# Attention of a hybrid trunk: value products of a unit in one block, probabilities divided by their sums on GpSimd

## The chip, the core and the metric

The kernel runs on one NeuronCore of a Trainium2 chip. The core has a matrix engine (TensorE, PE in the profile), VectorE (DVE), ScalarE (ACT), GpSimd (POOL) and a queue engine that issues most loads (SyncE, SP). Each engine takes its instructions strictly in the order in which they were put into its queue, and waits at semaphores for the others. Matrix products and transposes are written into PSUM (eight banks of 128 x 512 floats); GpSimd is given no PSUM operand anywhere in this kernel. The metric is the device time of one execution in microseconds (us).

## The reference, cut to what matters

Two trunk layers with three parallel mixers (pooling, gated linear attention, softmax attention), an output projection and an MLP, on 512 latent and 256 context tokens of width 1024. The change touches the softmax attention alone: 8 query heads of 64, which share 2 key/value heads.

```python
def gqa_attend(qb, k, v):
    s = jnp.einsum('bqhgd,bkhd->bhgqk', qb, k, preferred_element_type=jnp.float32) * HEAD_DIM ** -0.5
    p = jax.nn.softmax(s, axis=-1)
    return jnp.einsum('bhgqk,bkhd->bqhgd', p.astype(v.dtype), v)
...
    mix = jnp.concatenate([pool_mixer(p, w_pool, s_pool),
                           gla_output(o_gl, gg, g_gla, x.dtype),
                           latent_attention(ql, k_all, v_all)], axis=-1) @ w_out
```

Latent queries see all 768 keys (latent and context); context queries, which only the first layer has, see the 256 context keys.

## The kernel before

**Units.** The attention of a layer is cut into units: one pair of heads (`hp`, 0 to 3) times 256 queries. A latent unit (`q0` 0 or 2) has four tiles of 128 queries x 768 keys (two heads, two query blocks). A context unit (`q0` 4, first layer only) has four tiles of 128 x 256. The first layer has 8 latent and 4 context units, the second has 8 latent ones.

**Softmax part (L1009).** For each tile of a latent unit TensorE writes the scores into a PSUM buffer of two banks (`sc`, L1033 and L1034; the queries are held as high and low parts one above the other, so that the products with the high and the low part of the keys make up the whole). VectorE takes the row maximum (`nmx`, L1036), ScalarE the exponential, whose row sums come out beside it (`p` and `sm`, L1037). There are two such PSUM buffers (`psA`), so the scores of the tile after next wait for the exponential of this one. After the four tiles VectorE takes the reciprocal of the four sums (L1039). A context unit does the same with one PSUM tile for all four (L1019 to L1025).

**Value part (L1043).** The probabilities must lie with the keys on the partitions. For each block of 128 keys TensorE transposes the four tiles into one bank (`pT`, L1054), and ScalarE (even blocks, L1064) or VectorE (odd blocks, L1066) copies it to SBUF (`pe`). The blocks go in pairs: two blocks are transposed and copied, and then multiplied with the values of their keys into one accumulator (`av`, L1071; two products for each block, one for each head, into the upper and the lower 64 partitions). After the last pair four small matmuls spread the reciprocal sums over the partitions (`rb`, L1078), ScalarE copies the result (L1082), VectorE multiplies (`f`, L1084), ScalarE makes the high part of the mix (L1086) and GpSimd the low part (L1087). Each float32 matmul of `av` and `rb` appears as two instructions in the profile.

**Interleaving.** `att_thread` steps the softmax part of unit n and, after each step, one step of the value part of unit n-1: transposes and products of one pair beside each score tile, the end with `rb` beside the reciprocal. Before the first unit of a pair of heads, `q_stack` (L1093) transposes and splits the queries. In the early part of the attention the steps of gated linear attention run between (an order string, `STEPS`, says how); the pooling runs between the units. The framework puts the instructions into the queues by priority in the order of the program, with a timing estimate of its own, and sets all waits; the order within a queue is fixed before the run.

**Buffers.** The probability tiles take four of five buffers of the weight tags `hi` and `lo`, by turns. The copies `pe` of a pair share one tile of the tag `raw`, of which there are three, and which the weight loads use too (`wload`, L152). The copies of the last unit of a layer lie in other slots, so that the three `raw` buffers come free for the loads of the output projection's weights (`w_out`), which follow the attention. `psB` (one bank each: `pT`, `rb`, `qT`, `op`) has three buffers, the accumulator `av` has one. `sub_lo` (L78) is VectorE's subtraction that makes the low part of a split value.

Of the kernel before, what the change touches and what calls it, by code (L numbers as in the profile page):

```python
# [10 lines left out]
F32 = mybir.dt.float32  # L11
F32R = mybir.dt.float32r
I32 = mybir.dt.int32
AF = mybir.ActivationFunctionType
ALU = mybir.AluOpType
# [19 lines left out]
def hybrid_kernel(ctx, tc, x, c, cx, c_ctx, w_mod, b_mod, g_mix, w_in, w_pool, s_pool, w_gate, b_gate,  # L35
                  g_gla, g_q, g_k, w_out, g_mlp, w_up, w_down, g_final, k_mask, k_rope, k_edge, k_invw, out):
    nc = tc.nc
    V, A, G, T = nc.vector, nc.scalar, nc.gpsimd, nc.tensor
# [13 lines left out]
    def nm(s):  # L52
        uid[0] += 1
        return f"{s}_{uid[0]}"

    def slot(s, dt=F32, w=NT):
        return sp.tile([128, w], dt, tag="S", name=nm(s))
# [10 lines left out]
    def psA(s):  # L68
        return pa.tile([128, 1024], F32, tag="pa", name=nm(s))

    def psB(s):
        return pb.tile([128, 512], F32, tag="pb", name=nm(s))

    def psC(s):
        return pc.tile([128, 512], F32, tag="pc", name=nm(s))

    def sub_lo(lo, full, hi):
        V.tensor_tensor(lo, full, hi.bitcast(F32), ALU.subtract)  # L78
# [8 lines left out]
    ident = const.tile([128, 128], F32, name="ident")  # L87
# [336 lines left out]
    for l in range(2):  # L424
# [434 lines left out]
        def vview(t, kv):  # L859
            return UVt[0][:, t * 128 + kv * 64:t * 128 + kv * 64 + 64]  # L860
# [144 lines left out]
        def ptiles(n):  # L1005
            tag = "lo" if n % 2 else "hi"
            return [wp.tile([128, 1024], F32, tag=tag, name=nm("p"))[:, 0:NT] for _ in range(4)]

        def softmax_part(n, hp, q0, P):  # L1009

            kh, kl = kst[hp // 2]
            sm = mp.tile([128, 4], F32, tag="sm", name=nm("sm"), bufs=4)
            nmx = mp.tile([128, 4], F32, tag="nmx", name=nm("nmx"), bufs=4)
            if q0 == 4:
                sc_ = psA("scc")
                for i in range(4):
                    lq = qst[2 * hp + i // 2][:, NL + (i % 2) * 128:NL + (i % 2) * 128 + 128]
                    sv = sc_[:, i * NC:(i + 1) * NC]
                    T.matmul(sv, lq, kh[:, NL:NT], start=True, stop=False)  # L1019
                    T.matmul(sv, lq, kl[:, NL:NT], start=False, stop=True)  # L1020
                V.tensor_reduce(nmx, sc_.rearrange("p (t k) -> p t k", t=4), AX.X, ALU.max, negate=True)
                yield
                pts = [t_[:, j * NC:(j + 1) * NC] for t_ in (slot("pcx", w=2 * NC), slot("pcx", w=2 * NC)) for j in range(2)]
                for i in range(4):
                    A.activation(pts[i], sc_[:, i * NC:(i + 1) * NC], AF.Exp, bias=nmx[:, i:i + 1], accum_out=sm[:, i:i + 1])  # L1025
            else:
                pts = ptiles(n)
                for i in range(4):
                    c0 = (q0 + i % 2) * 128
                    lq = qst[2 * hp + i // 2][:, c0:c0 + 128]  # L1030
                    sc_ = psA("sc")
                    for z0, zn in ((0, NL), (NL, NC)):
                        T.matmul(sc_[:, z0:z0 + zn], lq, kh[:, z0:z0 + zn], start=True, stop=False)  # L1033
                        T.matmul(sc_[:, z0:z0 + zn], lq, kl[:, z0:z0 + zn], start=False, stop=True)  # L1034
                    sv = sc_[:, 0:NT]
                    V.tensor_reduce(nmx[:, i:i + 1], sv, AX.X, ALU.max, negate=True)  # L1036
                    A.activation(pts[i], sv, AF.Exp, bias=nmx[:, i:i + 1], accum_out=sm[:, i:i + 1])  # L1037
                    yield
            V.reciprocal(sm, sm)  # L1039
            P.extend((pts, sm))  # L1040
            yield

        def value_part(n, hp, q0, P):  # L1043
            pts, sm = P
            mhi, mlo = mixT[4 + hp]
            kts = [4, 5] if q0 == 4 else list(range(6))
            av_ = psC("av")

            for k0 in range(0, len(kts), 2):
                pes = []  # L1050
                for ki in (k0, k0 + 1):
                    pt_ = psB("pT")
                    for i, p_ in enumerate(pts):
                        T.transpose(pt_[:, i * 128:(i + 1) * 128], p_[:, ki * 128:(ki + 1) * 128], ident)  # L1054
                    pes.append(pt_)
                for ki, pt_ in zip((k0, k0 + 1), list(pes)):
                    if nunits - 1 - n < 1:
                        pe = slot("pe", w=512)
                    else:
                        if ki == k0:  # L1060
                            wide_ = wp.tile([128, 1024], F32, tag="raw", name=nm("pe"), bufs=3)
                        pe = wide_[:, (ki - k0) * 512:(ki - k0 + 1) * 512]
                    if ki % 2 == 0:
                        A.activation(pe, pt_, AF.Copy)  # L1064
                    else:
                        V.tensor_copy(pe, pt_)  # L1066
                    pes[ki - k0] = pe
                for ki, pe in ((k0 + 1, pes[1]), (k0, pes[0])):
                    vst = vview(kts[ki], hp // 2)
                    for hh in range(2):  # L1070
                        T.matmul(av_[64 * hh:64 * hh + 64, 0:256], vst, pe[:, hh * 256:hh * 256 + 256],  # L1071
                                 start=(ki == 1), stop=(ki == len(kts) - 2))
                yield

            rb_ = psB("rb")
            for i in range(2):
                for hh in range(2):
                    T.matmul(rb_[64 * hh:64 * hh + 64, i * 128:(i + 1) * 128],  # L1078
                             sm[:, 2 * hh + i:2 * hh + i + 1].to_broadcast([128, 64]), ident, start=True, stop=True)
            f = slot("f", w=512)  # L1080
            rb = f[:, 256:512]
            A.activation(rb, rb_[:, 0:256], AF.Copy)  # L1082
            f = f[:, 0:256]
            V.tensor_tensor(f, av_[:, 0:256], rb, ALU.mult)  # L1084
            ms = slice(q0 * 128, q0 * 128 + 256)
            A.activation(mhi[:, ms], f, AF.Copy)  # L1086
            G.tensor_tensor(mlo[:, ms], f, mhi[:, ms].bitcast(F32), ALU.subtract)  # L1087
            yield

        pool_ = pool_thread()  # L1090
# [17 lines left out]
        def att_thread():  # L1108
            k_transposes()
            k_stack(0)  # L1110
            q_stack(0)
            yield
            k_stack(1)
            yield
            nonlocal nunits
            units = [(hp, q0) for hp in range(4) for q0 in ((0, 2, 4) if both else (0, 2))]
            nunits = len(units)
            prev = iter(())
            for n, (hp, q0) in enumerate(units):
                P = []  # L1120
                for i, _ in enumerate(softmax_part(n, hp, q0, P)):
                    next(prev, None)
                    yield
                run(prev)
                if q0 == 0 and hp < 3:
                    q_stack(hp + 1)
                prev = value_part(n, hp, q0, P)
                next(pool_, None)
                yield
            yield from prev  # L1130
            run(pool_)
# [210 lines left out]
```

## Time and profile before

| | |
|---|---|
| time, median of 3 runs (all) | 1676.79 us (1674.35, 1676.79, 1676.84) |
| the profiled execution | 1671.28 us, its span 1669.1 us |
| granted TensorE clock, mean | 0.985 |
| attention, first layer (scores of the first unit to products of the last) | about 228 to 369 us |
| attention, second layer | about 1140 to 1256 us |
| matmuls of `av` / transposes of `pT` / matmuls of `rb` | 416 / 416 / 160 |

A row of a group reads: line, engine, operation, written tile<-read tiles, shapes, count | busy us in total, mean ns of one | idle time of the engine just before them, and what ended it. In the chain of waits each row is a start in us, a duration and what ran; it follows from the end of the run back to what released each step. In the timeline a row is a start, a duration, the engine, the line and the operation, with the idle time before it in brackets.

### The profile page before, as it was taken

How to read it: one execution, taken by the hardware profiler on the slowest of the kernel's cores; microseconds unless marked ns; L12 is line 12 of the kernel's file. 1: busy time of each engine (PE TensorE's matmuls, PEld its weight loads, DVE VectorE, ACT ScalarE, POOL GpSimd, SP SyncE). 2: the span in 40 equal slices, each digit the busy share in tenths (PEclk: the TensorE clock that was granted, in tenths of full speed). 3: DMA queues.
4: the chain of work that ended last, by engine and by line, in shares of the span. 5: the costliest groups of instructions: out<-in, count | busy, mean ns of one | idle time of the engine just before them, and what ended most of it. 6: DMA issues, size and time to landing. Idle time of an engine off the chain costs nothing.

```text
span 1669.1 us, 27434 instructions
## 1 busy us (share of the span) xinstructions
PE 1595.7 (96%) x11403; PEld 1306.2 (78%) x11403; DVE 923.3 (55%) x1330; ACT 630.9 (38%) x1074; POOL 406.4 (24%) x476
## 2 busy tenths in 40 slices
PE   7999979999999999999999999897999999999997
PEld 4888856678888888888888789785667888888886
DVE  5437666753673654636546563587763545455554
ACT  5545445561531312213113234555662523223332
POOL 1121311212303041130321462241201122222224
PEclk9999989999999999999999999998999999999999
DMA  9445400222340422515424332100032313333331
GB/s 330 128 135 175 149 2 7 98 93 59 102 139 26 141 97 59 176 50 172 150 65 170 103 108 81 40 2 2 33 121 75 111 54 101 101 101 101 101 101 51
DMA packets 136636, 163.31 MB, mean 98 GB/s; under 512 B 9908, under 2 KB 108608, under 8 KB 136512
## 3 DMA queue, kind: packets, MB, share of 16 engines
q1 hardware_dynamic: 130176, 148.41, 27.9%
q10 hardware_dynamic: 5824, 13.12, 2.1%
q8 instruction: 89, 1.46, 0.4%
q14 instruction: 35, 0.29, 0.1%
q0 software_dynamic: 512, 0.03, 0.0%
HBM read 157.31 MB, written 4.23 MB: 97 GB/s over the span
## 4 chain that ended last, share of the span: by engine, by line
PE 84%; DVE 6%; ACT 4%; DMA 2%; issue 2%; POOL 2%; SPq 0%; ACTq 0%; DVEq 0%; POOLq 0%
PE dn L340 25%; PE up L321 19%; PE tm L340 7%; PE op L340 6%; PE up L323 5%; PE fm L321 4%; PE av L1071 3%; PE pT L1054 2%; PE up L330 2%; PE fm L323 1%; PE sc L1033 1%; PE att L769 1%; PE sc L1034 1%; DVE nmx L1036 1%; PE pm L190 1%
## 5 line engine op out<-in xcount | busy, mean ns | idle before, releaser
L159 ACT ACTIVATE whi<-raw 128x1024 fp32r<-128x1024 f32 (+2 forms) x182 | 185.3, 1033 | 568.0 <-PE dn L340 293.0
L1194 POOL TENSOR_TENSOR X<-X,rtmp 128x512 f32<-128x512 f32 x158 | 216.1, 1370 | 640.4 <-DVE rtmp L1193 640.1
L78 DVE TENSOR_TENSOR wlo<-raw,whi 128x1024 fp32r<-128x1024 f32 (+2 forms) x182 | 223.6, 1237 | 213.4 <-ACT whi L159 211.7
L1193 DVE TENSOR_TENSOR rtmp<-dn,ga 128x512 f32<-128x512 f32 x160 | 109.5, 689 | 212.8 <-PE dn L340 211.3
L340 PE MATMUL dn<-whi,ah 128*128 128x512 f32 x480 | 187.3, 390 | 0.6 <-ACT whi L159 0.6
L340 PE MATMUL dn<-whi,al 128*128 128x512 f32 x480 | 187.2, 390 | 0.0
L340 PE MATMUL dn<-wlo,ah 128*128 128x512 f32 x480 | 186.2, 390 | 0.0
L321 PE MATMUL up<-h2h,whi 128*128 128x512 f32 x464 | 182.5, 393 | 1.5 <-ACT relu L1240 1.5
L321 PE MATMUL up<-h2h,wlo 128*128 128x512 f32 x464 | 182.9, 394 | 0.0
L321 PE MATMUL up<-h2l,whi 128*128 128x512 f32 x464 | 182.4, 393 | 0.0
L340 PEld LDWEIGHTS dn<-whi,ah 128*128 128x128 f32 x480 | 90.1, 188 | 22.0 <-ACT whi L159 1.0
L321 PEld LDWEIGHTS up<-h2h,whi 128*128 128x128 f32 x464 | 87.1, 188 | 24.1 <-ACT relu L1240 1.7
L340 PEld LDWEIGHTS dn<-wlo,ah 128*128 128x128 f32 x480 | 90.1, 188 | 19.5 <-DVE wlo L78 0.5
L340 PEld LDWEIGHTS dn<-whi,al 128*128 128x128 f32 x480 | 90.1, 188 | 19.4
L340 PE MATMUL tm<-whi,hTh 128*128 128x256 f32 (+1 forms) x352 | 102.3, 292 | 1.1 <-ACT UV L891 1.1
L321 PEld LDWEIGHTS up<-h2h,wlo 128*128 128x128 f32 x464 | 87.1, 188 | 19.6
L321 PEld LDWEIGHTS up<-h2l,whi 128*128 128x128 f32 x464 | 87.1, 188 | 19.3
L340 PE MATMUL tm<-whi,hTl 128*128 128x256 f32 (+1 forms) x352 | 100.7, 287 | 0.0
L340 PE MATMUL dn<-whi,a 128*128 128x512 f32 x320 | 100.0, 395 | 0.4 <-DVE rtmp L1193 0.4
L340 PE MATMUL tm<-wlo,hTh 128*128 128x256 f32 (+1 forms) x352 | 100.2, 288 | 0.0
L229 DVE SCALAR_TENSOR_TENSOR macc<-rawm,sstat,macc 128x1024 f32<-128x1024 f32 x56 | 76.3, 1383 | 8.2 <-DMA rawm<-in_w_mod_dram 7.7
L1036 DVE TENSOR_REDUCE nmx<-sc 128x1 f32<-128x768 f32 x64 | 60.5, 955 | 24.1 <-PE sc L1034 23.3
(293 smaller groups left out, 3320.6 us busy)
## 6 DMA issues: line engine op xcount, KB each, us to landing
rawm<-in_w_mod_dram SPq DMA_DIRECT2D x80, 512.0 KB, 5.2
raw<-in_w_up_dram SPq DMA_DIRECT2D x64, 512.0 KB, 4.5
raw<-in_w_down_dram SPq DMA_DIRECT2D x64, 512.0 KB, 4.6
raw<-in_w_in_dram SPq DMA_DIRECT2D x26, 512.0 KB, 3.9
rawm<-in_w_mod_dram SPq DMA_DIRECT2D x32, 256.0 KB, 5.3
raw<-in_w_out_dram SPq DMA_DIRECT2D x16, 512.0 KB, 4.7
raw<-in_w_in_dram SPq DMA_DIRECT2D x12, 256.0 KB, 2.8
ga<-gaD ACTq DMA_DIRECT2D x6, 512.0 KB
```

The costliest lines, as they stand in the source:

```text
L78: V.tensor_tensor(lo, full, hi.bitcast(F32), ALU.subtract)
L159: A.activation(hi, raw, AF.Copy)
L229: V.scalar_tensor_tensor(acc[s], raw, c_, acc[s], ALU.mult, ALU.add)
L321: T.matmul(ps[:, 0:NL], a, b[:, 0:NL], start=st, stop=sp_)
L323: T.matmul(ps[:, NL:NT], a, b[:, NL:NT], start=st, stop=sp_)
L330: T.matmul(ps[:, cs], a, b[:, cs], start=(k == 0 and i == 0), stop=(k == nk - 1 and i == 2))
L340: T.matmul(ps, a[:, sl], bb, start=(k == 0 and i == 0), stop=(k == nk - 1 and i == 2))
L1036: V.tensor_reduce(nmx[:, i:i + 1], sv, AX.X, ALU.max, negate=True)
L1054: T.transpose(pt_[:, i * 128:(i + 1) * 128], p_[:, ki * 128:(ki + 1) * 128], ident)
L1071: T.matmul(av_[64 * hh:64 * hh + 64, 0:256], vst, pe[:, hh * 256:hh * 256 + 256], start=(ki == 1), stop=(ki == len(kts) - 2))
L1193: V.tensor_tensor(tmp, ps, ga[0 if t < 4 else 1][:, sl], ALU.mult)
L1194: (V if b == NB - 1 and not both and t == 3 else G).tensor_tensor(X[t][:, sl], X[t][:, sl], tmp, ALU.add)
```

## The change

The reciprocal of a tile's sum is taken as soon as its exponential is done, and GpSimd multiplies the whole tile of probabilities by it in place, one tensor_scalar for each tile (128 x 768, or 128 x 256 in a context unit). The transposes read the multiplied tiles. The value part first transposes and copies all blocks of keys, one pair a step as before, and then runs all value products of the unit in one block; the last block of keys goes first into the accumulator. The four `rb` matmuls, the copy of their result and the multiplication `f` are gone. The high part of the mix is taken from the accumulator directly, and the low part too, by VectorE (`sub_lo`) in place of GpSimd.

```diff
--- before.py
+++ after.py
@@ -1023,6 +1023,9 @@
                 pts = [t_[:, j * NC:(j + 1) * NC] for t_ in (slot("pcx", w=2 * NC), slot("pcx", w=2 * NC)) for j in range(2)]
                 for i in range(4):
                     A.activation(pts[i], sc_[:, i * NC:(i + 1) * NC], AF.Exp, bias=nmx[:, i:i + 1], accum_out=sm[:, i:i + 1])
+                V.reciprocal(sm, sm)
+                for i in range(4):
+                    G.tensor_scalar(pts[i], pts[i], sm[:, i:i + 1], None, ALU.mult)
             else:
                 pts = ptiles(n)
                 for i in range(4):
@@ -1035,25 +1038,27 @@
                     sv = sc_[:, 0:NT]
                     V.tensor_reduce(nmx[:, i:i + 1], sv, AX.X, ALU.max, negate=True)
                     A.activation(pts[i], sv, AF.Exp, bias=nmx[:, i:i + 1], accum_out=sm[:, i:i + 1])
+                    V.reciprocal(sm[:, i:i + 1], sm[:, i:i + 1])
+                    G.tensor_scalar(pts[i], pts[i], sm[:, i:i + 1], None, ALU.mult)
                     yield
-            V.reciprocal(sm, sm)
-            P.extend((pts, sm))
+            P.extend(pts)
             yield
 
         def value_part(n, hp, q0, P):
-            pts, sm = P
+            pts = P
             mhi, mlo = mixT[4 + hp]
             kts = [4, 5] if q0 == 4 else list(range(6))
             av_ = psC("av")
 
+            pes = {}
             for k0 in range(0, len(kts), 2):
-                pes = []
+                pts_ = []
                 for ki in (k0, k0 + 1):
                     pt_ = psB("pT")
                     for i, p_ in enumerate(pts):
                         T.transpose(pt_[:, i * 128:(i + 1) * 128], p_[:, ki * 128:(ki + 1) * 128], ident)
-                    pes.append(pt_)
-                for ki, pt_ in zip((k0, k0 + 1), list(pes)):
+                    pts_.append(pt_)
+                for ki, pt_ in zip((k0, k0 + 1), pts_):
                     if nunits - 1 - n < 1:
                         pe = slot("pe", w=512)
                     else:
@@ -1064,27 +1069,17 @@
                         A.activation(pe, pt_, AF.Copy)
                     else:
                         V.tensor_copy(pe, pt_)
-                    pes[ki - k0] = pe
-                for ki, pe in ((k0 + 1, pes[1]), (k0, pes[0])):
-                    vst = vview(kts[ki], hp // 2)
-                    for hh in range(2):
-                        T.matmul(av_[64 * hh:64 * hh + 64, 0:256], vst, pe[:, hh * 256:hh * 256 + 256],
-                                 start=(ki == 1), stop=(ki == len(kts) - 2))
+                    pes[ki] = pe
                 yield
-
-            rb_ = psB("rb")
-            for i in range(2):
+            order_ = [len(kts) - 1] + list(range(len(kts) - 1))
+            for j, ki in enumerate(order_):
+                vst = vview(kts[ki], hp // 2)
                 for hh in range(2):
-                    T.matmul(rb_[64 * hh:64 * hh + 64, i * 128:(i + 1) * 128],
-                             sm[:, 2 * hh + i:2 * hh + i + 1].to_broadcast([128, 64]), ident, start=True, stop=True)
-            f = slot("f", w=512)
-            rb = f[:, 256:512]
-            A.activation(rb, rb_[:, 0:256], AF.Copy)
-            f = f[:, 0:256]
-            V.tensor_tensor(f, av_[:, 0:256], rb, ALU.mult)
+                    T.matmul(av_[64 * hh:64 * hh + 64, 0:256], vst, pes[ki][:, hh * 256:hh * 256 + 256],
+                             start=(j == 0), stop=(j == len(kts) - 1))
             ms = slice(q0 * 128, q0 * 128 + 256)
-            A.activation(mhi[:, ms], f, AF.Copy)
-            G.tensor_tensor(mlo[:, ms], f, mhi[:, ms].bitcast(F32), ALU.subtract)
+            A.activation(mhi[:, ms], av_[:, 0:256], AF.Copy)
+            sub_lo(mlo[:, ms], av_[:, 0:256], mhi[:, ms])
             yield
 
         pool_ = pool_thread()
```

## Prediction

> **What bounds the kernel now.** I read the page first, then the stretches of the attention, then the chain of waits inside it.
>
> ```profile
> span 1669.1 us, 27434 instructions
> PE 1595.7 (96%) x11403; PEld 1306.2 (78%) x11403; DVE 923.3 (55%) x1330; ACT 630.9 (38%) x1074; POOL 406.4 (24%) x476
> PE 84%; DVE 6%; ACT 4%; DMA 2%; issue 2%; POOL 2%; SPq 0%; ACTq 0%; DVEq 0%; POOLq 0%
> ```
>
> TensorE is busy for 96% of the span and carries 84% of the chain. GpSimd is busy for a quarter, so there is room on it. A share of the whole run doesn't price a change to one stage, so I cut the attention into stretches (columns: stretch, its length, busy us of PE, weight loads, DVE, ACT, POOL, then granted clock).
>
> ```profile
> 230.00:260.00 30.00, 23.83 (x450) 18.06 (x450) 20.96 (x37) 16.81 (x42) 2.12 (x8) 0.75 0.01 2
> 320.00:350.00 30.00, 30.00 (x213) 21.93 (x214) 21.42 (x31) 21.16 (x50) 2.93 (x4) 0.94 0.01 1
> ```
>
> ```profile
> 1150.00:1185.00 35.00, 28.74 (x546) 21.07 (x546) 27.74 (x62) 22.49 (x54) 3.56 (x6) 1.00 0.01 2
> 1200.00:1240.00 40.00, 39.94 (x315) 29.99 (x317) 27.90 (x43) 27.32 (x58) 6.77 (x7) 1.00 0.24 93
> 1240.00:1260.00 20.00, 17.64 (x106) 12.67 (x103) 9.28 (x11) 7.60 (x11) 3.09 (x3) 1.00 0.56 185
> ```
>
> Three kinds of stretch. **Early** (230 to 260, 1150 to 1185), beside the linear attention, PE is at 79 and 82% and DVE at 70 and 79%: latency and DVE decide. **Steady** (320 to 350, 1200 to 1240) PE is full and DVE is at about 70%. **Tail** (1240 to 1260): PE at 88%, waiting for weights, as shown below. What PE no longer does is gained in the steady part, hardly in the early one. The chain there gives PE's prices:
>
> ```profile
> 1171.14 1.88 PE av L1071 x16
> ...
> 1235.11 1.02 PE av L1071 x8
> 1236.13 0.59 PE pT L1054 x4
> 1236.71 0.23 PE sc L1033
> 1236.94 0.23 PE sc L1034
> 1237.17 0.12 PE sc L1033
> 1237.29 0.12 PE sc L1034
> 1237.41 0.44 PE pT L1054 x4
> 1237.85 1.01 PE av L1071 x8
> 1238.86 0.44 PE rb L1078 x8
> ```
>
> A score tile costs 0.70 us (four rows), four transposes 0.44 behind scores but 0.59 behind `av`, a pair's products 1.01, and two pairs back to back 1.88 instead of 2 x 1.01. So every separate block of `av` costs about 0.14 + 0.15 = 0.29 us beyond its products: a price of changing between transposes and these half-width products.
>
> **The change part by part.**
>
> *One block of products.* Three blocks of a latent unit become one: two changes saved, 2 x 0.29 = 0.58 us. There are 16 latent units. A context unit has only one pair and saves nothing.
>
> *No spread.* `rb` goes: 0.44 us of PE for each of the 20 units. A latent unit then costs PE 4 x 0.70 + 6 x 0.44 + (1.01 + 2 x 0.87) + 0.15 = 8.34 us, against 9.36 before; the shed is 1.02, and 0.44 in a context unit. All of it on the path would be 16 x 1.02 + 4 x 0.44 = 18.1 us, the bound on the gain.
>
> *What the other engines get* (groups of 1170 to 1262: count, then busy us, mean ns, idle before):
>
> ```profile
> L1036 DVE TENSOR_REDUCE nmx<-sc 128x1 f32<-128x768 f32 x24 | 22.5, 954 | 7.0 <-PE sc L1034 6.8
> L1037 ACT ACTIVATE p<-sc,nmx 128x768 f32<-128x768 f32 x24 | 21.6, 900 | 10.5 <-DVE nmx L1036 10.4
> L1066 DVE COPY pe<-pT 128x512 f32<-128x512 f32 x19 | 13.1, 687 | 3.6 <-PE pT L1054 3.4
> L1037 ACT ACTIVATION_READ_ACCUMULATOR p<-sc,nmx 128x1 f32 x24 | 4.7, 196 | 0.0
> L1084 DVE TENSOR_TENSOR f<-av,f 128x256 f32<-128x256 f32 x7 | 3.0, 425 | 6.8 <-PE av L1071 5.3 <-ACT f L1082 1.5
> L1039 DVE RECIPROCAL sm<-sm 128x4 f32<-128x4 f32 x6 | 1.0, 175 | 2.1 <-ACT p L1037 2.1
> ```
>
> ACT loses the copy of `rb`. DVE exchanges `f` for the low part of the mix, the same shape from the same accumulator, 0.425 for 0.425. It gets four reciprocals of one column for one of four; I price each at the row's 0.175, since it is nearly all fixed cost, so 3 x 0.175 = 0.53 us more. DVE's latent unit goes from 4 x 0.954 + 3 x 0.687 + 0.175 + 0.425 = 6.48 to 7.00 us: from 69% of PE's unit to 84%. Each reciprocal waits for its exponential and the reading of its sum; queued behind it on DVE are the next maximum and the copies, for which ACT and PE wait. That is the cost of the new wait. Each is bounded by 0 (DVE had nothing else) and 0.9 + 0.2 us (the whole exponential, if the reciprocal stands ahead of the next maximum); four a unit.
>
> *GpSimd's multiplication* has no row of its own. The nearest:
>
> ```profile
> L842 POOL TENSOR_TENSOR mixl<-ogl,mixh 128x768 fp32r<-128x768 f32 x2 | 3.9, 1940 | 3.0 <-ACT sq L875 1.7 <-ACT mixh L841 1.3
> L602 POOL COPY KK<-KK 128x768 f32<-128x768 f32 x4 | 3.7, 915 | 59.5 <-ACT KK L601 59.5
> L959 POOL COPY pl<-pm 128x256 f32<-128x256 f32 x2 | 0.8, 400 | 0.0
> ```
>
> It streams one tensor, as the copy does (0.92 us); with two tensors it is 1.94. I take 1.1, near the copy, and keep both ends. Four make 4.4 us a unit, under PE's 8.34, and 7.8 at the upper end; the low part of the mix leaves it. In a context unit it is 4 x 0.4 to 0.5 by the narrow copy. GpSimd's throughput is no bound at either end; its latency may be.
>
> The Trainium skill (GPSIMD Engine Reference, section Performance versus the Vector engine) speaks against such a move: elementwise work takes GpSimd about twice VectorE's time, which, were it to hold for one input, is the upper end here and the second rival below; its table in Engine selection excepts one-input operations, as the copy's row does.
>
> *The longer way of the last tile.* From the end of the last scores of a unit to its transposes stand maximum 0.95, exponential 0.90, reading 0.20, reciprocal 0.18, multiplication 1.1, and five hand-overs of about 0.05: 3.6 us, where it was 2.0 (maximum, exponential, three hand-overs). PE has as cover the previous unit's block of products (2.75 + 0.15) and two score tiles of the next unit (2 x 0.70): 4.3 us. The margin of 0.7 is one DVE copy (0.687) ahead of the last maximum. So I expect no stall in the mean, but a frequent one. With DVE at 84% I take off 0.4 us a unit (an estimate between nothing and the whole 1.02), so 0.62 stays.
>
> At the first unit of a layer there is no cover:
>
> ```profile
> 245.44 0.90 PE L1054 MATMUL pT<-ident,p 128*128 128x128 f32 x3 [2.66 <-ACT p L1037]
> ```
>
> ```profile
> 1150.09 0.55 PE L1054 MATMUL pT<-ident,p 128*128 128x128 f32 x3 [1.08 <-ACT p L1037]
> ```
>
> Both fills get 1.6 us more, 3.2 together. DVE's work for the linear attention goes on meanwhile, so I count half, 1.6.
>
> *Buffers held longer.* The accumulator now takes its first product from the last key block, so no product can start before the last copy, and the three `raw` buffers of the last unit that uses them come free together, late. The loads of `w_out` wait for them:
>
> ```profile
> 1236.21 16.98 SPq L152 DMA_DIRECT2D raw<-in_w_out_dram  x8
> ```
>
> ```profile
> 1242.52 4.44 DMA raw<-in_w_out_dram
> ...
> 1247.95 0.59 ACT pe L1064
> ```
>
> The first load goes out at 1236.21, just when the first pair's products end (1235.11 + 1.02). In the new order there stand before that release four transposes, a score tile, four transposes, a copy, and three blocks of products: 1235.1 + 0.44 + 0.70 + 0.44 + 0.7 + 0.65 = 1238.0, some 1.9 us later. In the second layer this load is on the chain, and ACT's split of the weights stands ahead of the last unit's copies, which PE awaits. The other two buffers come about as early as before, so I count 1.5 there and 1.0 in the first layer: 2.5, between 0 and 3.8.
>
> **Sum.** Steady latent units: 16 less one early unit in the first layer, three early ones in the second and its last, so 11 x 0.62 = 6.8. Context units 4 x 0.44 = 1.8. Against it: fills 1.6; reciprocals in the four early units, 4 x 0.53 by DVE's 79% share there, 1.6; tails 2.5. Net 8.6 - 5.7 = 2.9 us less. The span becomes 1666.2; the profiled execution of 1671.28 (2.2 around the span) would be 1668.4. That execution lies 5.5 below the median of the runs shown, 1676.79; the same difference makes the median 1673.9.
>
> **The rivals.**
>
> *The whole shed is kept* (17%): nothing stalls in the steady part, 11 x 1.02 + 1.8, half of the other five units' 1.02 (2.6), less the tails: 15.6 - 2.5 = 13.1 less, 1663.7. For it: PE full in both steady stretches, two score buffers and three `psB` buffers as slack. Against it: DVE at 84%, and no margin on the last tile.
>
> *Transposes wait for GpSimd* (25%), the slower side. Place: the first transposes of each unit. It decides from the point where multiplication plus DVE's delay pass 1.8 us (4.3 - 3.6 + 1.1). With a multiplication of 1.9 and a last maximum one copy late the stall is about 0.8 us, and with a reciprocal in front of a maximum the 1.02 of the shed is used up: steady gain 0, fills in full with the longer multiplication 2 x 2.4 = 4.8, reciprocals 1.6, tails 2.5, context -1.8: 7.1 slower, 1683.9. For it: GpSimd is slowed beside VectorE where that reads two SBUF tensors:
>
> ```profile
> 1234.57 0.73 POOL L1087 TENSOR_TENSOR mixl<-f,mixh 128x256 fp32r<-128x256 f32 x1 [9.21 <-ACT mixh L1086]
> ...
> 1241.28 1.22 DVE L78 TENSOR_TENSOR wlo<-raw,whi 128x1024 fp32r<-128x1024 f32 x1
> ...
> 1242.02 1.07 POOL L1087 TENSOR_TENSOR mixl<-f,mixh 128x256 fp32r<-128x256 f32 x1 [6.72 <-ACT mixh L1086]
> ```
>
> The same operation took 1.07 instead of 0.73 beside such a subtraction. Against it: in the steady part DVE reads mostly PSUM.
>
> *The tails take it back* (8%): the weights arrive a whole load late behind ACT's split in both layers, 6 us instead of 2.5; net about 0.6 slower, 1677.4.
>
> **How the numbers follow.** The forecast has 50%, with an own range of -9 to +1 us. A difference under 0.2% (3.4 us) can't be told from none for this kernel. The forecast splits into 25% faster, 24% within, 1% slower; the full shed is 17% faster; the wait for GpSimd 4% within and 21% slower; the tails 6% and 2%. Together 42, 34 and 24%. The range goes from the full shed (1663) to a little past the wait for GpSimd (1685).
>
> **What would show it.** Right: no `rb`, products in runs of 24 at about 2.75 us, latent units 8.5 to 9 us apart in the steady part, PE still near 100% there, multiplications near 1.1 us. Wrong towards slower: idle time before `pT` put down to POOL, or a POOL multiplication near 1.9; DVE idle before reciprocals while a maximum waits. The tails: the first `w_out` load about 2 us later against the scores of the last unit, and PE idle before `op`. If PE's idle time in the steady part doesn't grow at all, the estimate of 0.4 is wrong and the full shed holds.

## The result, and the profile after

| | before | changed |
|---|---|---|
| median (lowest to highest), same chip | 1675.57 us (1673.1 to 1676.84) | 1712.78 us (1709.89 to 1714.56) |
| ratio, 95% interval | | 1.0227 [1.0214, 1.0241] |
| first layer: first scores to last, then to the first product with `w_out` | 228.4 to 351.1, 363.8 | 230.2 to 362.8, 384.3 |
| second layer, the same | 1139.0 to 1237.1, 1248.6 | 1160.9 to 1271.7, 1289.8 |

The change costs 2.3%: 38 us by the ratio, where 2.9 less was forecast and the range ended at 1685. The stage marks say where the two profiled executions part (spans 1669.1 and 1712.8, 43.7 apart): the two attentions take 9.9 and 12.7 us more between first and last scores, and the tails up to the projection 8.8 and 6.6. The rest is 1.8 and 1.4 us ahead of the two attentions and 2.5 behind the second layer's tail.

The page of the kernel after: its head and engine times, then its row of the multiplication.

```profile
span 1712.8 us, 27256 instructions
...
PE 1601.5 (94%) x11243; PEld 1311.6 (77%) x11243; DVE 932.6 (54%) x1378; ACT 623.6 (36%) x1054; POOL 548.3 (32%) x536
...
L1042 POOL TENSOR_SCALAR p<-p,sm 128x768 f32<-128x768 f32 x64 | 145.2, 2284 | 41.0 <-DVE sm L1041 32.4
```

One multiplication takes 2.28 us, not 1.1: more than the forecast's upper bound. Yet GpSimd is busy for only 32% of the span, so again it is the stage that has to be looked at. Two stretches of the kernel after (columns as in the prediction):

```profile
320.00:350.00 30.00, 22.71 (x140) 16.23 (x139) 20.63 (x37) 16.57 (x39) 25.52 (x19) 1.00 0.01 3
...
1240.00:1270.00 30.00, 25.20 (x172) 18.35 (x172) 20.39 (x39) 18.62 (x40) 30.00 (x16) 1.00 0.15 61
```

In 320 to 350 PE was busy for all 30 us before and is now for 22.7; GpSimd went from 2.9 to 25.5, and at the end of the second layer it is busy without a break. That looks like a bound on GpSimd: four times 2.28 is 9.1 us, more than PE's 8.34 a unit. The chain of waits, at the end of the first layer's attention, agrees:

```profile
359.08 10.94 POOL p L1042 x5
370.02 3.78 issue
...
373.85 3.64 POOL pcx L1028 x4
...
377.53 0.44 PE pT L1059 x2
377.97 1.47 PE av L1078 x12
...
379.50 3.66 DMA raw<-in_w_out_dram
...
384.29 17.87 PE op L340 x71
```

Five multiplications back to back, then, after 3.78 us that the profile puts down to nothing, those of a context unit; only then the last transposes and products, which free the `raw` buffers for the weights. One view doesn't fit, the waits of PE in 230 to 350 (what waited, for what: us in all, times, longest):

```profile
PE sc L1036 <- ACT p L1040: 6.6, 10, 1.5
PE pT L1059 <- ACT pe L1069: 2.8, 5, 0.7
...
PE pT L1059 <- POOL p L1042: 1.9, 2, 1.0
```

Transposes hardly wait for GpSimd. PE waits instead for score buffers, ahead of `sc`, for an exponential that GpSimd has no part in, though not much longer than the kernel before did (6.6 and 4.2 us in this stretch). If GpSimd's step is what costs, its price stands elsewhere than where its result is read; the experiments had to find where.

### The profile page after: what moved, and what is told of

The parts are those of the page before. It is cut to its first block, busy times and chain, and to the rows that moved or that the text cites. A ratio compares the mean times of both kernels' runs of the same rounds, so it can differ in the third digit from the quotient of the medians.

```text
span 1712.8 us, 27256 instructions
## 1 busy us (share of the span) xinstructions
PE 1601.5 (94%) x11243; PEld 1311.6 (77%) x11243; DVE 932.6 (54%) x1378; ACT 623.6 (36%) x1054; POOL 548.3 (32%) x536
## 3 DMA queue, kind: packets, MB, share of 16 engines
q8 instruction: 88, 1.44, 0.3%
## 4 chain that ended last, share of the span: by engine, by line
PE 79%; DVE 8%; ACT 5%; DMA 3%; POOL 3%; issue 2%; SPq 0%; ACTq 0%; DVEq 0%; POOLq 0%
PE dn L340 24%; PE up L321 19%; PE tm L340 7%; PE op L340 6%; PE up L323 5%; PE fm L321 4%; PE av L1078 2%; PE up L330 2%; DVE nmx L1039 1%; PE fm L323 1%; PE pT L1059 1%; DMA rawm<-in_w_mod_dram 1%; ACT p L1040 1%; PE att L769 1%; PE pm L190 1%
## 5 line engine op out<-in xcount | busy, mean ns | idle before, releaser
L1042 POOL TENSOR_SCALAR p<-p,sm 128x768 f32<-128x768 f32 x64 | 145.2, 2284 | 41.0 <-DVE sm L1041 32.4
L1059 PE MATMUL pT<-ident,p 128*128 128x128 f32 x384 | 63.5, 301 | 20.5 <-ACT pe L1069 11.6
```

The source lines that it names most:

```text
L1042: G.tensor_scalar(pts[i], pts[i], sm[:, i:i + 1], None, ALU.mult)
```

## The experiments

Three theories were held in turn: GpSimd's latency ahead of the transposes, GpSimd's throughput, and at last the order of the instructions. Ratios are to the kernel before, timed beside them on the same chip; the intervals are of 95%.

### The parts of the change (e1 to e4)

e1_dve: the multiplications go to VectorE.

```diff
-                    G.tensor_scalar(pts[i], pts[i], sm[:, i:i + 1], None, ALU.mult)
+                    V.tensor_scalar(pts[i], pts[i], sm[:, i:i + 1], None, ALU.mult)
```

> The changed kernel with the multiplications on VectorE in place of GpSimd; all else as changed. Theory G (GpSimd's 2.2 us for each of 64 multiplications, four a unit, is what costs 37 us): most of the loss goes, VectorE needs under 1 us for one, 1668 to 1688 us. Theory B (the single block of products, which takes TensorE's small fillers away and holds the raw buffers longer, is what costs): it stays above 1700 us, since VectorE is only loaded more.

e2_block: the kernel before, with only the order of the products taken from the change.

```diff
-                for ki, pe in ((k0 + 1, pes[1]), (k0, pes[0])):
+            order_ = [len(kts) - 1] + list(range(len(kts) - 1))
+            for j, ki in enumerate(order_):
...
```

> The kernel before with only the single block of products: sums spread by matmuls and multiplied at the end as before, no multiplication of the probabilities. Theory G: no loss, 1664 to 1677 us (0.58 us for each of 16 latent units saved, up to 3 us lost in the tails). Theory B: most of the loss is here, 1690 to 1712 us.

e3_mult: the changed kernel with the products by pairs as before (e2's edit the other way round).

> The changed kernel with the products by pairs, as before the change: the probabilities are multiplied by GpSimd, nothing is spread, and the products follow each pair of transposes. Theory G: the loss stays, 1700 to 1720 us. Theory B: the loss goes, under 1685 us.

e4_none: the changed kernel with no division.

```diff
-                    V.reciprocal(sm[:, i:i + 1], sm[:, i:i + 1])
-                    G.tensor_scalar(pts[i], pts[i], sm[:, i:i + 1], None, ALU.mult)
```

> The changed kernel without the reciprocals and without the multiplications: the division by the sums is left out. It shows what the single block and the missing spread are worth by themselves. Theory G: faster than the kernel before, 1655 to 1668 us. Theory B: slower than it, above 1685 us.

| | median us | ratio |
|---|---|---|
| e1_dve | 1686.11 | 1.0082 [1.0067, 1.0097] |
| e2_block | 1680.34 | 1.0044 [1.0027, 1.0061] |
| e3_mult | 1698.88 | 1.0168 [1.0150, 1.0187] |
| e4_none | 1665.39 | 0.9959 [0.9945, 0.9974] |

The division does the harm: without it the kernel is 0.4% faster than before, with it on GpSimd 2.3% slower. VectorE takes 0.657 us for the same multiplication, as the groups of e1_dve show, and the division costs 1.2 points over e4_none there too, with its reciprocals and whatever else the framework then lays out otherwise:

```profile
L1042 DVE TENSOR_SCALAR p<-p,sm 128x768 f32<-128x768 f32 x64 | 42.0, 657 | 1.2
```

The block of products isn't the gain it was taken for; alone it costs 0.4%. Two results lie outside the ranges of both theories: e2_block between them, e3_mult just under theory G's.

### How much division, and how the block is ordered (e5 to e8)

e5_pairs: e4_none with the products by pairs. e6_half: GpSimd multiplies half of the columns only (`pts[i][:, 0:384]`, and 128 of 256 in a context unit). e7_recip: the reciprocals stay, the multiplication goes. e8_natural: e2_block with the blocks of keys in their own order:

```diff
-            order_ = [len(kts) - 1] + list(range(len(kts) - 1))
+            order_ = list(range(len(kts)))
```

> The kernel before with the division left out altogether (no reciprocals, no spread, no multiplication), products by pairs. If the single block saves what its two changes of mode less per unit are worth (0.58 us each, 9 us), this is slower than the run without division with the block (1665): 1668 to 1674 us. If the block costs by itself, as the run of the block alone says (8 us more), it is faster: 1654 to 1662 us.

> The changed kernel with GpSimd multiplying only half of the columns of each tile (384 of 768, 128 of 256 in context units); the other half is left undivided. One multiplication should take about 1.25 us. If each us of multiplication costs in proportion (45 us for 2.2), 1688 to 1695 us. If the loss comes from GpSimd's throughput (four at 2.2 us are over TensorE's 8.3 us a unit), half is under the bound and the loss nearly goes: 1668 to 1680 us.

> The changed kernel with the reciprocals of each tile but without the multiplications: the division is left out. If VectorE waiting at its reciprocals costs much, 1674 us or more; if they are nearly free, as without them: 1665 to 1669 us.

> The kernel before with only the single block, but its products in the order of the keys, so that the first may start before the last copy and fill a gap. If it is the rule 'last key block first' that makes the block cost 8 us, this is back at 1664 to 1675 us; if the block costs because the products stand late in the order at all, it stays at 1678 to 1684 us.

| | median us | ratio |
|---|---|---|
| e5_pairs | 1664.96 | 0.9954 [0.9939, 0.9969] |
| e6_half | 1677.52 | 1.0031 [1.0014, 1.0049] |
| e7_recip | 1667.82 | 0.9979 [0.9966, 0.9992] |
| e8_natural | 1675.27 | 1.0019 [1.0009, 1.0030] |

With no division at all, pairs and one block come out alike (0.9954 and 0.9959): the block saves nothing (both lie in the gap between the two ranges given for e5_pairs). e8_natural comes out at the upper end of its first range. All of the division before is worth 0.46%, some 7.7 us, about the most that another way of dividing can gain while the framework lays out the order. And e7_recip is the changed kernel with everything but the multiplication: 0.2% faster, 3.5 us. About 41 us come with the multiplication. e6_half's row is 1307 ns, so 5.2 us a unit:

```profile
L1042 POOL TENSOR_SCALAR p<-p,sm 128x384 f32<-128x384 f32 x64 | 83.2, 1307 | 83.0 <-DVE sm L1041 61.6
```

Half the work costs about 9 us over e7_recip, and all of it about 41. A loss that rises so steeply where four multiplications pass PE's unit looked like a bound on GpSimd's throughput. It was the wrong conclusion.

### A shorter step on GpSimd, and half the load (e9 to e12)

e9_copy puts a GpSimd copy of each tile onto itself in the multiplication's place, e10_imm a multiplication by a constant. e11_split gives every other tile to VectorE. e12_early is an attempt at a faster kernel, on the tail.

```diff
-                    G.tensor_scalar(pts[i], pts[i], sm[:, i:i + 1], None, ALU.mult)
+                    G.tensor_copy(pts[i], pts[i])                                                        # e9_copy
+                    G.tensor_scalar(pts[i], pts[i], 1.0, None, ALU.mult)                                 # e10_imm
+                    (G if i % 2 else V).tensor_scalar(pts[i], pts[i], sm[:, i:i + 1], None, ALU.mult)    # e11_split
```

```diff
-                    if nunits - 1 - n < 1:
+                    if nunits - 1 - n < 1 or (nunits - 1 - n < 2 and k0 == 0):
                         pe = slot("pe", w=512)
```

> The changed kernel with a GpSimd copy of each tile onto itself in place of the multiplication, behind the same reciprocal: the division is left out of the computation. The page of before has GpSimd's copy of 128x768 at 0.92 us, near the 1.1 us of the forecast. Theory (GpSimd's work in a unit, four times the multiplication, is what decides; nothing much happens below the 8.3 us of PE's unit): 3.7 us a unit cost less than the 5.2 us of e6_half (1677.5), and more than none at all (e7_recip, 1667.8): 1670 to 1676, so the forecast of 1673.9 would about have held with the multiplication at the forecast's price. Rival (any step of GpSimd between exponential and transposes costs PE its hand-overs, and the port that it shares): close to e6_half or above it, 1677 or more, though the row is short.

> The changed kernel with GpSimd multiplying each tile by the constant 1.0 in place of the column of reciprocals: the division is left out of the computation. If the column of scalars makes the multiplication slow, the row drops from 2.2 us to near the copy's 0.92, and the time to that of e9_copy, 1670 to 1676. If it is the arithmetic instruction itself on GpSimd, the row stays at 2.2 us and the time at that of the changed kernel, 1706 to 1713.

> The changed kernel with the tiles shared out: of each four, the first and third are multiplied by VectorE and the second and last by GpSimd. The last tile still waits the whole 2.2 us for GpSimd ahead of the transposes, as in the changed kernel, but GpSimd has 2 x 2.2 = 4.4 us a unit in place of 9. Theory (GpSimd's throughput): with 4.4 us GpSimd costs no more than in e6_half (1677.5), and VectorE's two multiplications about half of what four cost in e1_dve (1686): 1676 to 1687, GpSimd idle between its pairs. Rival (the latency of the last tile's multiplication ahead of the transposes): that is unchanged, so 1700 to 1711.

> The kernel before, with one edit of another place: the first pair of copies of the unit before the last takes two slots of the common pool rather than a raw buffer, so that the raw buffers come free earlier for the loads of w_out. The page of before has that load on the chain at 1242.52, 4.44 us, and PE waiting for the weights at the end of each layer's attention. If the load's start is what holds the tail, it goes out 2 to 4 us earlier and PE's first product with w_out follows 1 to 2.5 us earlier in each layer: 1667 to 1671 beside 1672.3 for the kernel before. If the slots of the common pool or the other two raw buffers hold it, no change within 2 us.

| | median us | ratio |
|---|---|---|
| e9_copy | 1701.31 | 1.0159 [1.0143, 1.0174] |
| e10_imm | 1710.48 | 1.0208 [1.0191, 1.0225] |
| e11_split | 1687.78 | 1.0080 [1.0065, 1.0095] |
| e12_early | 1674.02 | 1.0002 [0.9992, 1.0011] |

e11_split falls a little past the upper end of the throughput theory and well short of the latency rival. e9_copy is far outside. The copy takes 0.84 us, less than the forecast's price, and the multiplication by a constant 2.14. The groups of e9_copy, then of e10_imm:

```profile
L1042 POOL COPY p<-p 128x768 f32<-128x768 f32 x64 | 53.9, 841 | 105.8 <-ACT p L1040 101.5 <-PE sc L1037 3.8
```

```profile
L1042 POOL TENSOR_SCALAR p<-p 128x768 f32<-128x768 f32 x64 | 135.7, 2137 | 46.8 <-ACT p L1040 45.8 <-DVE pe L1071 0.6
```

In 230 to 350 GpSimd has room with the copy, while PE is no better off than in the changed kernel. The one row of that stretch, first of e9_copy, then of the kernel after:

```profile
230.00:350.00 120.00, 91.05 (x924) 66.02 (x925) 79.33 (x150) 58.98 (x141) 40.34 (x71) 0.89 0.10 37
```

```profile
230.00:350.00 120.00, 93.73 (x926) 68.15 (x927) 81.04 (x154) 59.78 (x141) 80.31 (x69) 0.86 0.10 37
```

GpSimd at 40 of 120 us, PE idle for 29; GpSimd at 80, PE idle for 26. So throughput fell as the main cause: e6_half, with a step of 1.31 us, takes 1677.5 us, and e9_copy, with one of 0.84, takes 1701.3. The framework lays out the queues before the run, and what was left to suspect was the order itself.

The next expectation says that e9_copy and e10_imm have one order. The traces show that they don't. PE behind the same four matmuls of the linear attention, in e9_copy and then in e10_imm:

```profile
249.52 0.48 PE L769 MATMUL att<-QQ,KK 64*64 64x64 f32 x4 [3.48 <-DVE KK L726]
249.93 0.90 PE L1059 MATMUL pT<-ident,p 128*128 128x128 f32 x3
```

```profile
258.03 0.48 PE L769 MATMUL att<-QQ,KK 64*64 64x64 f32 x4 [3.50 <-DVE KK L726]
258.44 0.79 PE L1036 MATMUL sc<-kh,qs 128*128 128x512 f32 x1
```

An alignment of the two sequences leaves some 160 of PE's 11243 instructions in another place. So the 9 us between these two runs are not the price of the longer step alone, and e9_copy, whose order is that of no other run, can't tell order from duration.

### The order and the step, each alone (e13 to e16)

e7_recip and the changed kernel issue the same instructions on PE, VectorE and ScalarE; only their order differs. In these four kernels the order on the three engines is given: each instruction gets its predecessor in the wanted queue as an order edge (no semaphore). In the traces e13_order and e16_copy_order have on these engines, instruction by instruction, the sequence of e7_recip, and e14_late that of the changed kernel. All rows of the three engines then bear line 48, a helper that notes the instructions; the multiplication is L1292.

```diff
+    V, A, T = Keep(nc.vector, REC["DVE"]), Keep(nc.scalar, REC["ACT"]), Keep(nc.tensor, REC["PE"])
...
+        for x, y in zip(o, o[1:]):
+            tc.add_manual_dep(ins[y], ins[x].name, mybir.DependencyInfo(
+                mybir.DependencyClass.NoSync, mybir.DependencyReason.DATA), reason="order")
```

> The changed kernel, with all its multiplications on GpSimd, but TensorE, VectorE and ScalarE take their instructions in the order that e7_recip has (the same instructions, laid out with no multiplication ahead of the transposes). Theory (the order that the framework lays out for a slow GpSimd step is what costs; e9_copy and e10_imm have one order and GpSimd times of 0.84 and 2.14 us, and differ by 9 us only): most of the loss over e7_recip (1667.8) goes, 1672 to 1688. Rival (GpSimd's time, by throughput or latency): the engines still wait for 2.2 us four times a unit, 1698 to 1712, and PE's idle time before transposes is put down to POOL.

> The other way round: e7_recip, so no multiplication at all (the division is left out of the computation, the reciprocals stay), but TensorE, VectorE and ScalarE take their instructions in the order of the changed kernel. Theory (order): the loss stays though GpSimd has nothing to do, 1690 to 1705. Rival (GpSimd's time): with no GpSimd step there is no loss, 1666 to 1674.

> e3_mult (products by pairs as before, multiplications on GpSimd), with TensorE, VectorE and ScalarE in the order that the same kernel has when its multiplications are left out. A whole computation, and a candidate for the fastest. Theory (order): e5_pairs has 1665 without any division, reciprocals cost some 2 us, and GpSimd's time what e13_order shows: 1670 to 1685, against 1698.9 for e3_mult. Rival (GpSimd's time): 1692 to 1700.

> e9_copy (a GpSimd copy of 0.84 us in place of each multiplication; the division is left out) in the order of e7_recip. It is what the forecast took for the multiplication, about, in an order that doesn't plan for more. Theory (order): 1668 to 1674, against 1701 for e9_copy. Rival (GpSimd's hand-overs or port): 1690 or more, as e9_copy.

| GpSimd's step | early order (of e7_recip) | late order (of the changed kernel) |
|---|---|---|
| none | e7_recip, 1667.82, 0.9979 | e14_late, 1706.32, 1.0199 [1.0184, 1.0215] |
| copy, 0.84 us | e16_copy_order, 1679.55, 1.0039 [1.0024, 1.0054] | not run (e9_copy, in an order of its own: 1701.31, 1.0159) |
| multiplication, 2.3 us | e13_order, 1751.78, 1.0475 [1.0454, 1.0495] | changed kernel, 1712.78, 1.0227 |

e15_pairs_order, the same for pairs, gave 1722.31, 1.0297 [1.0265, 1.0330], against 1.0168 for e3_mult: slower, in neither theory's range. e16_copy_order lies between the two ranges given for it.

e14_late settles the first half. Nothing stands between the exponential and the transposes there, and the kernel still loses 2.0% (a little past the upper end of the order theory's range, far from the rival's). In the changed kernel the multiplication itself adds only 1.0227 - 1.0199 to that, about 5 us, with intervals that just touch; nearly all of the loss is taken by the order. Its row for 230 to 350, then that of e7_recip:

```profile
230.00:350.00 120.00, 95.68 (x946) 70.26 (x948) 78.56 (x154) 61.39 (x145) 14.91 (x34) 0.86 0.10 37
```

```profile
230.00:350.00 120.00, 101.11 (x1024) 76.54 (x1024) 86.25 (x171) 68.51 (x159) 15.46 (x34) 0.91 0.10 37
```

The timeline of PE in e14_late shows two kinds of waits (start, duration, instruction, idle time before it):

```profile
324.42 0.40 PE L48 MATMUL sc<-kh,qs 128*128 128x512 f32 x1
...
325.11 0.27 PE L48 MATMUL pT<-ident,p 128*128 128x128 f32 x1
326.84 0.50 PE L48 MATMUL sc<-kh,qs 128*128 128x512 f32 x1 [1.45 <-ACT p L48]
...
335.99 2.15 PE L48 MATMUL pT<-ident,p 128*128 128x128 f32 x13
338.50 0.33 PE L48 MATMUL pT<-ident,p 128*128 128x128 f32 x1 [0.36 <-DVE pe L48]
339.10 2.81 PE L48 MATMUL av<-pe,UV 128*64 128x256 f32 x24 [0.27 <-DVE pe L48]
```

Score tiles follow each other with one transpose between, and there are two score buffers, so a third score tile waits for an exponential. The transposes, planned late, come in runs of 13, and in the runs PE waits for the copies of `pT`. The early order has such places too: in 230 to 350 its score products wait 5.6 us for `p`, those of e14_late 6.5. What each kind of wait adds is seen in the whole run. The groups of the transposes and of the first score products, of e7_recip and then of e14_late:

```profile
L1056 PE MATMUL pT<-ident,p 128*128 128x128 f32 x384 | 58.6, 285 | 8.2 <-DVE pe L1068 2.4 <-ACT p L1038 2.4 <-ACT pe L1066 2.3
L1034 PE MATMUL sc<-kh,qs 128*128 128x512 f32 x64 | 34.1, 534 | 14.7 <-ACT p L1038 6.9 <-ACT kh L998 3.5 <-DVE dg L789 2.9
```

```profile
L48 PE MATMUL pT<-ident,p 128*128 128x128 f32 x384 | 63.8, 303 | 17.8 <-ACT pe L48 11.0 <-DVE pe L48 5.5 <-DVE qs L48 0.7
L48 PE MATMUL sc<-kh,qs 128*128 128x512 f32 x64 | 35.4, 552 | 21.0 <-ACT p L48 12.0 <-ACT kh L48 3.6 <-DVE dg L48 1.8
```

Transposes wait 16.5 us for copies instead of 4.7, score products 12.0 us for exponentials instead of 6.9. With all other waits PE is idle (span less busy time) for 104.3 us instead of 82.1: 22.2 of the 37.6 us between the two profiled executions. The other 15.4 us are no waiting. PE is busy for longer with the same instructions, as the two pages say, e7_recip and then e14_late:

```profile
PE 1584.9 (95%) x11243; PEld 1303.1 (78%) x11243; DVE 926.3 (56%) x1378; ACT 622.9 (37%) x1054; POOL 392.4 (24%) x456
```

```profile
PE 1600.3 (94%) x11243; PEld 1313.9 (77%) x11243; DVE 929.1 (55%) x1378; ACT 623.7 (37%) x1054; POOL 388.9 (23%) x456
```

The mean granted clock was 0.982 and 0.972. In 1156 to 1181 of e14_late it was 0.50, and a transpose took 417 ns (median); in 1215 to 1240 it was 1.00, and a transpose took 273. So the late order is paid for in waits and in slower matmuls. That PE's idle time brings the lower clock about is likely, but no run here separates the two.

e13_order answers the other half, against its expectation: in the early order the slow multiplication costs 83 us over e7_recip (1.0475 - 0.9979), where the rival, GpSimd's time, gave at most 45. Of the 84.8 us between the profiled spans, PE is busy for longer in 33.4, at a mean clock of 0.957. The waits are where one looks for them. PE's waits in 230 to 350, and two of them in its timeline:

```profile
PE pT L48 <- POOL p L1292: 16.9, 10, 4.2
PE pT L48 <- POOL pcx L1278: 3.9, 2, 3.7
```

```profile
341.64 0.33 PE L48 MATMUL pT<-ident,p 128*128 128x128 f32 x1 [1.32 <-POOL p L1292]
...
342.51 0.47 PE L48 MATMUL sc<-kh,qs 128*128 128x512 f32 x1
...
347.60 0.48 PE L48 MATMUL pT<-ident,p 128*128 128x128 f32 x1 [4.15 <-POOL p L1292]
```

The transpose of one tile stands right behind the scores of the next ones. PE's queue is strict, so the scores behind it, which show no wait of their own, are held up too. So the late order hides GpSimd's step, and with a step of 2.3 us it is 2.5 points (41 us) better than the early one. With a step of 0.84 us the early order (1679.6) is better than the one that the framework laid out (1701.3).

Not tried: an order between the two, the copy in the late order, and the time of a version with the order written out by hand for a step of 2.3 us. No whole computation among these beat the kernel before; e12_early equals it.

## Why the prediction was wrong, point by point

**What bounds the kernel: right.** PE is the bound in the steady part of the kernel before, and the loss stands on PE. Its idle time went from 73.4 to 111.3 us. Its busy time, which should have fallen with the 160 products of `rb`, went from 1595.7 to 1601.5, at a mean clock of 0.985 and 0.972.

**The shed of PE: too large, one of its two parts is missing.** For a kernel without any division the forecast's prices give 11 x 1.02 + 1.8 = 13.0 us, 10.5 after its tails; e4_none has 0.41% (6.9 us). The 0.44 us a unit for the spread fits: 15 x 0.44 = 6.6, and e5_pairs, which saves the spread and keeps the pairs, has 0.46% (7.7 us). The 0.58 us a unit put down to fewer changes between transposes and products brings nothing: e4_none, with the block, gains no more than e5_pairs. With the spread kept, the block alone costs 0.4% (e2_block), and 0.2% when the first product may start before the last copy (e8_natural). That the last block of keys goes first was seen in the prediction, but priced in the tails alone. That e7_recip, 3.5 us faster, comes near the forecast's 2.9 is luck: it has no step on GpSimd, for which the forecast had taken off 6.0 (11 x 0.4 and 1.6 at the fills).

**Reciprocals: not contradicted.** 1.6 us forecast; e7_recip lies 0.2 points (3.3 us by the ratios) above e4_none, with an interval about as wide.

**GpSimd's multiplication: the first step that failed.** "I take 1.1, near the copy, and keep both ends", 0.92 and 1.94. It was 2.28, outside both, and with a constant in place of the column of reciprocals 2.14, so the arithmetic is what costs, not the column. The argument that it "streams one tensor, as the copy does" is wrong on these rows. "GpSimd's throughput is no bound at either end" fails with it: 9.1 us a unit is above 8.34, and GpSimd ran without a break from 1240 to 1270. The sentence on the Trainium skill (GPSIMD Engine Reference, section Performance versus the Vector engine: about twice VectorE's time) pointed the right way; measured, it is 2284 to 657 ns, 3.5 times, so this one-input work is no exception.

**The cover: the step that decided.** "PE has as cover the previous unit's block of products (2.75 + 0.15) and two score tiles of the next unit": 4.3 us against 3.6. That counted with the order that the program's text suggests, a unit's transposes all behind its last tile. The queues have the transposes tile by tile between the scores of the same unit, so the cover is a score tile or two. At about the price that the forecast took, the step is too small as well: with 0.84 us e16_copy_order lies 0.6 points (10 us) above e7_recip in the same order, where 6.0 had been taken off, and e9_copy with the framework's own order 30. And the order was taken as fixed: that a new step lets the framework lay out all the other engines' work anew was priced at nothing. That is 37 of the 41 us by which the changed kernel lies above e7_recip (e14_late against e7_recip, 1.0199 - 0.9979): more waits of PE, for copies and exponentials, and slower matmuls.

**Tails: the right place, a wrong size and a wrong cause.** 2.5 us forecast, 8.8 and 6.6 seen. The first load of `w_out` does go out later: 7.1 us after and 0.9 before the last scores in the kernel before, 16.7 and 6.8 us after them now. The forecast's sum of 1.9 us for this had three blocks of products at 0.65; by its own prices they are 1.44, which gives 2.7, and e7_recip, with the same block order, has 2.7 and 2.9. But the load isn't what holds the tail of the kernel before: in e12_early it goes out 3 us earlier in both layers against the last scores, and the first product with `w_out` doesn't come earlier by more than 0.3. The tails come with the order: 15.0 and 7.0 us in e7_recip (12.7 and 11.5 before), 19.8 and 17.9 in e14_late, 21.5 and 18.0 in the changed kernel. Behind the last scores of the two layers stand 31 and 22 transposes in e7_recip, 50 and 45 in e14_late.

**The rivals.** "Transposes wait for GpSimd" had the right engine, at a price a fifth of what came: 7.1 us slower. It counted the stall at the first transposes of each unit; it didn't count that the framework avoids this stall by another order, which costs more. The signs named there half held: the multiplication past 1.9 us was in the page, PE's idle time before `pT` put down to POOL hardly was (1.9 us in 230 to 350), since in this order the waits stand before other instructions. VectorE's idle time before the reciprocals was there, 21.4 us in the whole run, but e7_recip has 20.4 of it and isn't slow.

## What to carry to other kernels

Where a framework lays out the queues, a new step between a producer and a consumer is priced twice, by its own duration and by the new order of everything beside it; give a kernel the other kernel's order to tell the two apart, and compare the orders in the traces before a difference is put down to the step's duration. A step that the critical engine's queue must wait for is covered by what stands between the two instructions in that queue, to be read from the timeline of the trace and not from the loops of the program. And the saving in view (here about 7.7 us) sets how much a replacement may cost.

## What the runs showed of the hardware

- GpSimd's multiplication of a 128 x 768 float tile by one scalar a row took 2.28 us, by a constant 2.14, of 128 x 384 1.31 (e6_half); its copy of 128 x 768 in place took 0.84, VectorE's multiplication 0.66.
- With one and the same order on the three other engines, GpSimd busy for 80.31 us rather than 14.91 in 230 to 350 (the changed kernel and e14_late) cost about 5 us in the whole run: what its work takes from the other engines, by waits and by sharing anything with them, comes to that in sum.
- In e14_late a 128 x 128 float transpose took 417 ns (median) where the granted clock was 0.50, and 273 where it was 1.00. With the same 11243 instructions PE was busy for 1584.9 us at a mean clock of 0.982 (e7_recip), 1600.3 at 0.972 (e14_late) and 1618.3 at 0.957 (e13_order).
